# Alternating the row strips of small matmuls, a block-diagonal compression and nested expert conditions in a two-block transformer step

## The chip, the cores and the metric

One Trainium2 chip; the program runs on one core. The metric is the device time of one execution in microseconds (us), the median of several runs.

## The reference

One sequence of 256 tokens of width 1024 goes through two blocks, all in float32.

The first block adds a mix of two branches (a two-direction RWKV-7 scan over a context of 256 tokens and then the sequence; a two-dimensional neighbourhood attention) and then a mixture of 16 experts, of which each token takes two. The second block is two layers. Each projects its input to the operands of four branches, mixes their outputs by gates and adds a feed-forward step over a table of 128 x 128 experts. Two of the four branches matter here:

```
# sparse attention: 15 compressed keys and values, from 32 tokens each
tok = jnp.arange(n_cmp)[:, None] * CMP_STRIDE + jnp.arange(CMP_LEN)[None, :]
def compress(kv, w):
    blk = kv[:, tok] + cmp_pos
    return blk.reshape(B, n_cmp, CMP_LEN * Dh) @ w
kc = compress(k_cmp, cmp_wk)
vc = compress(v_cmp, cmp_wv)
...
# gated linear attention (GLA): 4 heads, 32 wide, chunked
att = jnp.einsum('bhtk,bhsk,bhtsk->bhts', qi, ki, decay)
intra = jnp.einsum('bhts,bhsv->bhtv', att, vi)
```

In the first block, the RWKV step needs, per head of width 64, the products of decayed keys with decayed keys and queries within chunks of 64 tokens.

## The kernel before

**Weights and products.** All weights stream from memory in float32, in units of 128 x 1024 (512 KB). Class `Stream` loads each unit into a tile wf (4 buffers, all loads issued by SyncE, SP in the profile, in the program's order) and splits it in two fp32r parts: wh by ScalarE, wl by VectorE or GpSimd. A dense product is then three matmuls (`mm3`, lines 418 to 420: high by high, low by high, high by low). Matmuls in plain float32, as the attention branches use them, leave two LDWEIGHTS and two MATMUL records each in the trace.

**Row strips.** A matmul whose contraction is 64 or 32 rows uses the strip of the array at its operands' partitions: head p in partitions 64p to 64p + 63, or, for GLA, head h in 32h to 32h + 31.

**Order.** Functions are generators; `interleave` (from line 340) runs them in turn, a step to each yield. In `layer` (around line 1690) three run side by side: the dense projections (za, zt, zb, zc and then the gate weights mg), one lane with stick-breaking and then sparse attention (`nsa`), one lane with `gla` and then retention. A lane waits until `self.ready` counts the projections that it needs; `ready` is 7 when the last, zc, is there. The framework's own scheduler then decides the order of instructions on each engine, so neighbours in the code need not stay neighbours on TensorE.

**The places of the change.**
- `rw_prep` (first block, L1050): for each of two strips p four matmuls into one bank, then masks by VectorE (L1053), then the next strip; behind both, transposes (L1057). It is called 16 times; in half of them the moving operand is 64 wide, in half 128.
- `moe`: the experts run with 64 slots each (`SLOTS`). Then a count n, the most tokens of one expert, is loaded to registers of all engines, and three conditions in a row (L1360: n over 64, 128, 192) guard three further passes; with the inputs here n is not over 64 and none is entered. Behind them mx = accumulated output x m5 (L1372) is added to x (L1374), and the layer norm (L1603) and transposes (L465) start the second block.
- `gla`: per head and per half tt of the tokens, 8 matmuls of 32 rows (L1869, one of the eight L1867) into banks 4 and 5, four to a bank; two multiplies by masks (L1872) and a sum (L1873); then a cross product (L1876).
- `nsa`: the compression weights cw (128 x 32 x 64, keys in partitions 0 to 63, values in 64 to 127) come in one load; per token offset j two matmuls accumulate: keys (L1920, 64 rows by 64, 15 moving columns, bank 2) and values (L1921, 64 rows by 15, 64 moving columns, bank 3). ScalarE copies the keys to kcb (L1925), VectorE the values to vcb (L1927). Further down the scores of the selected and window keys (L1976) loop over strip p, then over b.

## Time and profile before

| | |
|---|---|
| median of 3 runs | 3157.56 us (3152.04 to 3164.92) |
| the profiled execution | 3153.57 us |
| its span, first to last instruction | 3151.8 us, 52665 instructions |
| mean granted TensorE clock | 0.966 of full speed |
| TensorE (PE) busy | 2972.6 us, 94% |
| its weight loads (PEld) busy | 2544.3 us, 81% |
| VectorE (DVE) busy | 2028.2 us, 64% |
| ScalarE (ACT) busy | 1411.4 us, 45% |
| GpSimd (POOL) busy | 382.0 us, 12% |
| read from memory | 548.62 MB, 174 GB/s over the span |

The profile is of one execution. Its times are from the start of the span. Busy times of TensorE come from modelled ends of matmuls: starts that follow each other tell the pitch. [...] An "L" with a number is a line of the kernel before. Names: bank is an accumulator bank; X are GLA's decayed operands; blk the windows of 15 x 32 tokens; KBT and KRT the RWKV operands.

### The profile page before, as it was taken

To read this page: it belongs to the slowest core of one execution; us is meant where nothing else is said; L and a number is where in the kernel's file an instruction comes from. 1 tells how busy PE (TensorE), PEld (TensorE's weight loads), DVE (VectorE), ACT (ScalarE), POOL (GpSimd) and SP (SyncE) were. 2 spreads that over 40 slices of the span, in tenths; PEclk is the share of its full clock that TensorE was granted. 3 is DMA by queue.
4 is the path that set the end of the run, shared out by engine and by line. 5 is a ranking of instruction groups with operands and counts; after the bars stand their busy time and mean duration, and the time that the engine had idled before them with its cause. 6 is when DMAs were issued, how large, how long until landed. Compare 5 with 4: busy or idle time off the path is not lost. (4 is left out here: it accounts for less than half of the span.)

```text
span 3151.8 us, 52665 instructions
## 1 busy us (share of the span) xinstructions
PE 2972.6 (94%) x20690; PEld 2544.3 (81%) x20690; DVE 2028.2 (64%) x3822; ACT 1411.4 (45%) x2488; POOL 382.0 (12%) x334
## 2 busy tenths in 40 slices
PE   7999958899699989999999999999999999999998
PEld 5789647544388979999998888789889999988886
DVE  3568586311265577968986666664669868976666
ACT  4555433211254544444544555553444445445553
POOL 1110131000101051320010000110413310010000
PEclk9999968999899999999999999998999999999999
DMA  6333516699332444554445555533454554456665
GB/s 229 127 95 116 196 38 252 269 409 408 130 124 101 156 154 156 174 181 155 155 168 196 193 193 193 186 117 101 159 165 154 168 167 157 156 186 192 193 193 159
DMA packets 159134, 553.29 MB, mean 176 GB/s; under 512 B 19442, under 2 KB 25748, under 8 KB 157588
## 3 DMA queue, kind: packets, MB, share of 16 engines
q1 hardware_dynamic: 158868, 549.74, 50.6%
q8 instruction: 168, 2.75, 0.4%
q14 instruction: 98, 0.80, 0.1%
HBM read 548.62 MB, written 1.05 MB: 174 GB/s over the span
## 5 line engine op out<-in xcount | busy, mean ns | idle before, releaser
L337 DVE TENSOR_TENSOR wl<-wf,wh 128x1024 fp32r<-128x1024 f32 x690 | 865.9, 1255 | 402.2 <-ACT wh L336 401.4
L336 ACT CAST wh<-wf 128x1024 fp32r<-128x1024 f32 x745 | 778.6, 1046 | 682.0 <-PE bank L419 475.0
L420 PE MATMUL bank<-xth,wl 128*128 128x256 f32 x3040 | 869.5, 287 | 18.9 <-DVE wl L337 15.4
L418 PE MATMUL bank<-xth,wh 128*128 128x256 f32 x3040 | 884.6, 291 | 2.8 <-ACT B L2075 1.5
L419 PE MATMUL bank<-xtl,wh 128*128 128x256 f32 x3040 | 867.8, 286 | 2.9 <-DVE xtl L477 2.9
L420 PEld LDWEIGHTS bank<-xth,wl 128*128 128x128 f32 x3040 | 588.2, 194 | 23.1 <-DVE wl L337 17.7
L418 PEld LDWEIGHTS bank<-xth,wh 128*128 128x128 f32 x3040 | 588.7, 194 | 10.8 <-issue 2.1
L419 PEld LDWEIGHTS bank<-xtl,wh 128*128 128x128 f32 x3040 | 589.2, 194 | 4.3 <-DVE xtl L477 3.7
L419 PE MATMUL bank<-wl,gh 128*128 128x512 f32 x1024 | 399.0, 390 | 3.5 <-DVE wl L337 3.5
L420 PE MATMUL bank<-wh,gll 128*128 128x512 f32 x1024 | 396.2, 389 | 0.0
L418 PE MATMUL bank<-wh,gh 128*128 128x512 f32 x1024 | 278.2, 389 | 3.2 <-ACT gh L413 3.2
L413 ACT CAST gh<-B 128x256 fp32r<-128x256 f32 x256 | 103.6, 407 | 340.5 <-PE bank L419 340.5
L419 PEld LDWEIGHTS bank<-wl,gh 128*128 128x128 f32 x1024 | 192.2, 188 | 45.0 <-DVE wl L337 5.2
L418 PEld LDWEIGHTS bank<-wh,gh 128*128 128x128 f32 x1024 | 192.2, 188 | 43.6 <-ACT gh L413 3.6
L420 PEld LDWEIGHTS bank<-wh,gll 128*128 128x128 f32 x1024 | 192.2, 188 | 39.7
L414 DVE TENSOR_TENSOR gll<-B,gh 128x256 fp32r<-128x256 f32 x256 | 116.9, 459 | 130.1 <-ACT gh L413 127.4
L337 POOL TENSOR_TENSOR wl<-wf,wh 128x1024 fp32r<-128x1024 f32 (+1 forms) x55 | 153.1, 2786 | 312.0 <-ACT wh L336 303.8
L1445 PE MATMUL bank<-raw,xe 128*64 128x512 f32 x512 | 130.1, 600 | 0.0
L2280 DVE TENSOR_TENSOR eq<-iota,picks 128x1024 f16<-128x1024 f16 x128 | 89.4, 699 | 47.1 <-PE bank L2292 45.7
L506 POOL TENSOR_TENSOR x<-x,r_ln 128x1024 f32<-128x1024 f32 x12 | 34.8, 2930 | 500.1 <-DMA r_ln<-in_rows 489.4
L1445 PEld LDWEIGHTS bank<-raw,xe 128*64 128x64 f32 x512 | 37.2, 136 | 66.0 <-issue 64.2
L2281 DVE TENSOR_TENSOR gm<-eq,picks 128x1024 f16<-128x1024 f16 x128 | 88.6, 693 | 0.0
(588 smaller groups left out, 4370.1 us busy)
## 6 DMA issues: line engine op xcount, KB each, us to landing
wf<-in_pu SPq DMA_DIRECT2D x256, 512.0 KB, 3.5
wf<-in_pv SPq DMA_DIRECT2D x256, 512.0 KB, 4.2
raw<-in_w SPq DMA_DIRECT2D x192, 512.0 KB, 10.1
wf<-in_mg SPq DMA_DIRECT2D x64, 512.0 KB, 3.5
mw<-in_modw SPq DMA_DIRECT2D x48, 512.0 KB, 4.6
wf<-in_win_t SPq DMA_DIRECT2D x37, 512.0 KB, 3.6
wf<-in_wq SPq DMA_DIRECT2D x32, 512.0 KB, 3.6
wf<-in_zt SPq DMA_DIRECT2D x28, 512.0 KB, 3.3
```

The costliest lines, as they stand in the source:

```text
L336: nc.scalar.copy(h[:, :w], src[:, :w])
L337: (nc.gpsimd if gpsimd else nc.vector).tensor_sub(lo[:, :w], src[:, :w], h[:, :w])
L413: self.nc.scalar.copy(h, src)
L414: return self.nc.vector.tensor_sub(lo, src, h)
L418: mm(out, lh, rh, start=start, stop=False)
L419: mm(out, lh, rl, start=False, stop=False)
L420: return mm(out, ll, rh, start=False, stop=stop)
L506: nc.gpsimd.tensor_tensor(self.x[:, tt], self.x[:, tt], gb[:, a:a + D], op=op)
L1445: nc.tensor.matmul(self.ps[j][half[e]], v[p]["x"][:, kk, half[e]], w[j][e][:, c], start=kk == 0, stop=kk == KC - 1)
L2280: nc.vector.tensor_tensor(e, iota[:, None, None].to_broadcast(big), of(0), op=OP.is_equal)
L2281: nc.vector.tensor_tensor(g, e[:, :, 1:2].to_broadcast(big), of(1), op=OP.mult)
```

## The change

Three parts.

- **Heads in turn.** `rw_prep` takes both banks first and alternates the strip with each matmul; `gla` takes heads in pairs, one bank for each head of the pair, and alternates them with each matmul, with the multiplies of both heads behind; the score loop in `nsa` has strip p inside. In `gla` a wait for `ready` = 7 stands before the last step.
- **Compression as one product.** cw is padded on the host to a block-diagonal 128 x 128 per offset (2 MB per layer instead of 1), comes in four loads of eight offsets through two buffers, and 32 matmuls of 128 rows and 15 moving columns give keys and values in one bank. The values, now as 64 x 15, are copied out by VectorE (vt) and transposed by TensorE before the copies to vcb.
- **Conditions nested.** The second condition stands inside the first, the third inside the second (`beyond`).

```
-        o[f"cw_{l}"] = np.concatenate([i[n][l].reshape(32, 64, 64).transpose(1, 0, 2)
-                                       for n in ("nsa_cmp_wk_2", "nsa_cmp_wv_2")], 0)
+        o[f"cw_{l}"] = np.concatenate([np.pad(i[n][l].reshape(32, 64, 64).transpose(1, 0, 2), ((0, 0), (0, 0), (64 * q, 64 - 64 * q)))
+                                       for q, n in enumerate(("nsa_cmp_wk_2", "nsa_cmp_wv_2"))], 0)
...
+                pas = [bank().rearrange("p (c t) -> p c t", c=4) for _ in range(2)]
+                for c in range(4):
+                    for p in range(2):
+                        h = slice(p * 64, p * 64 + 64)
+                        nc.tensor.matmul(pas[p][:, c, :W], flat(KBT[h, c]), flat(KRT[h, c]), start=True, stop=True)
                 for p in range(2):
-                    h = slice(p * 64, p * 64 + 64)
-                    pa = bank().rearrange("p (c t) -> p c t", c=4)
-                    for c in range(4):
-                        nc.tensor.matmul(pa[:, c, :W], flat(KBT[h, c]), flat(KRT[h, c]), start=True, stop=True)
+                    h, pa = slice(p * 64, p * 64 + 64), pas[p]
...
-        for lo in range(SLOTS, T, SLOTS):
-            with tc.If(n > lo), tc.tile_pool(name=f"ex{lo}", bufs=1) as ep:
...
+        self.beyond(n, SLOTS)
...
+    def beyond(self, n, lo):
+        nc, tc = self.nc, self.tc
+        with tc.If(n > lo):
+            with tc.tile_pool(name=f"ex{lo}", bufs=1) as ep:
...
+            if lo + SLOTS < T:
+                self.beyond(n, lo + SLOTS)
...
+        for h0 in range(0, 4, 2):
+            rows = [slice(h * 32, h * 32 + 32) for h in (h0, h0 + 1)]
+            atts = [sp.tile([128, 3, 128], F32, name="att", bufs=2) for _ in rows]
             for tt in range(2):
                 t = slice(tt * 128, tt * 128 + 128)
+                tmps = [sp.tile([128, 8, 128], F32, name="tmp", bufs=2) for _ in rows]
                 for q in range(2):
+                    pq = [self.bank(4, 5).rearrange("p (a b) -> p a b", a=4) for _ in rows]
                     for j in range(4):
                         lv = 4 * q + j
+                        for pp, r in zip(pq, rows):
+                            if lv == at[tt][7]:
+                                nc.tensor.matmul(pp[:, j], kT[r, t], qT[r, t], start=True, stop=True)
+                            else:
+                                nc.tensor.matmul(pp[:, j], X[tt][r, lv], X[tt][r, lv], start=True, stop=True)
+                    yield
+                    for pp, tmp in zip(pq, tmps):
+                        nc.vector.tensor_tensor(tmp[:, 4 * q:4 * q + 4], pp, gm[:, 4 * q + 1 - tt:4 * q + 5 - tt], op=OP.mult)
...
+        while self.ready < 7:
+            yield
...
-        cw = self.load(sp, "cw", A[f"cw_{l}"])
+        some = lambda j: self.load(sp, "cw", A[f"cw_{l}"][:, j:j + 8], bufs=2)
+        cw = [some(0), some(8)]
...
         for j in range(32):
-            nc.tensor.matmul(pk[0:64, 0:15], cw[0:64, j], blk[0:64, j], start=j == 0, stop=j == 31)
-            nc.tensor.matmul(pv[64:79, 0:64], blk[64:128, j], cw[64:128, j], start=j == 0, stop=j == 31)
+            nc.tensor.matmul(pk[:, 0:15], cw[j // 8][:, j % 8], blk[:, j], start=j == 0, stop=j == 31)
             if j % 8 == 7:
+                if len(cw) < 4:
+                    cw.append(some(8 * len(cw)))
                 yield
+        vt = sp.tile([128, 15], F32, name="vt")
+        nc.vector.tensor_copy(vt[64:128], pk[64:128, 0:15])
...
+        nc.tensor.transpose(pv[0:15, 0:64], vt[64:128], self.ident[64:128, 64:128])
+        yield
         for h in range(4):
-            nc.vector.tensor_copy(vcb[h * 32:h * 32 + 15, h], pv[64:79, 0:64])
+            nc.vector.tensor_copy(vcb[h * 32:h * 32 + 15, h], pv[0:15, 0:64])
...
-                for p in range(2):
-                    for b in range(2):
+                for b in range(2):
+                    for p in range(2):
```

The change adds lines, so that a line of the kernel before has a higher number in it: the dense products 418 to 420 are 419 to 421, 1869 is 1880, 1920 and 1921 are 1939.

Three places show how the order of instructions moves. The first is TensorE's order in the first layer's GLA. A row is a line, an operation, its bank and operands, and "x3" three alike in a row; X0 and X1 are the two halves of the tokens. Before, the products of one head in the first half, dense products around them:

```order
L420 MATMUL bank1_62<-xth_10348,wl_10891 128x256
L1763 MATMUL bank6_67<-zA_10344,att_10875 128x64
L1869 MATMUL bank4_65<-X0_10586 128x128
L1764 MATMUL bank6_67<-zA_10344,att_10875 128x64
L1765 MATMUL bank6_67<-zA_10344,att_10875 128x64
L1869 MATMUL bank4_65<-X0_10586 128x128 x3
L1869 MATMUL bank5_66<-X0_10586 128x128 x3
L1867 MATMUL bank5_66<-zT_10347 128x128
L418 MATMUL bank0_61<-xth_10348,wh_10936 128x256
```

After, a group of the first pair of heads; bank 4 is the even head's, bank 5 the odd one's:

```order
L1880 MATMUL bank4_65<-X0_10586 128x128
L1880 MATMUL bank5_66<-X0_10586 128x128
L1880 MATMUL bank4_65<-X0_10586 128x128
L1880 MATMUL bank5_66<-X0_10586 128x128
L1880 MATMUL bank4_65<-X0_10586 128x128
L1880 MATMUL bank5_66<-X0_10586 128x128
L1880 MATMUL bank4_65<-X0_10586 128x128
L1880 MATMUL bank5_66<-X0_10586 128x128
L420 MATMUL bank1_62<-xtl_10349,wh_10907 128x256
```

and another of the same pair, in the second half of the tokens:

```order
L1774 MATMUL bank6_67<-zA_10344,att_10738 128x64
L1880 MATMUL bank4_65<-X1_10587 128x128 x4
L419 MATMUL bank1_62<-xth_10348,wh_10822 128x256
L420 MATMUL bank1_62<-xtl_10349,wh_10822 128x256
L1880 MATMUL bank5_66<-X1_10587 128x128 x4
L421 MATMUL bank1_62<-xth_10348,wl_10823 128x256
```

One group alternates the heads with each product, the other has the two heads apart with dense products between. In all a layer has, by strip, the groups 000, 11101, 00110101, 00001111, 0000, 1111, 23232323 and three times 22233323.

The second place is TensorE's order in the compression of the first layer. Before, keys (bank 2) and values (bank 3) alternate:

```order
L1921 MATMUL bank3_64<-cw_11433,blk_11435 15x64 x4
L1920 MATMUL bank2_63<-blk_11435,cw_11433 64x15
L1921 MATMUL bank3_64<-cw_11433,blk_11435 15x64
L1920 MATMUL bank2_63<-blk_11435,cw_11433 64x15
L1921 MATMUL bank3_64<-cw_11433,blk_11435 15x64
L1920 MATMUL bank2_63<-blk_11435,cw_11433 64x15
L1921 MATMUL bank3_64<-cw_11433,blk_11435 15x64
```

After, the 32 products stand in chunks of 1, 9, 2, 12 and 8 with dense products between; two of the chunks:

```order
L1757 MATMUL bank3_64<-lm_11311,c_ones_10842 128x128
L1939 MATMUL bank2_63<-blk_11440,cw_11436 128x15 x7
L1939 MATMUL bank2_63<-blk_11440,cw_11438 128x15 x2
L419 MATMUL bank0_61<-xth_10348,wh_11288 128x256
...
L421 MATMUL bank1_62<-xth_10348,wl_11359 128x256
L1939 MATMUL bank2_63<-blk_11440,cw_11438 128x15 x4
L1939 MATMUL bank2_63<-blk_11440,cw_11462 128x15 x8
L1774 MATMUL bank6_67<-zB_10345,att_11466 128x64
```

The third is SP's order of loads in the first layer, after the change (before, one load of cw, 128x2048, stands at the front and none further down):

```order
L386 DMA cpos<-in_cpos 128x32
L386 DMA cw<-in_cw 128x1024 x2
L284 DMA wf<-in_za 128x824 x4
...
L284 DMA wf<-in_mg 128x1024 x3
L386 DMA cw<-in_cw 128x1024
L284 DMA wf<-in_mg 128x1024 x3
L386 DMA cw<-in_cw 128x1024
L284 DMA wf<-in_mg 128x1024 x23
```

Two loads of cw stand ahead of the layer's weights, as the one did, and two among the gate weights mg.

## Rows read from the trace of the kernel before

**Rows 1.** The page's table of engines: busy us, share of the span, instructions.

```profile
PE 2972.6 (94%) x20690; PEld 2544.3 (81%) x20690; DVE 2028.2 (64%) x3822; ACT 1411.4 (45%) x2488; POOL 382.0 (12%) x334
```

**Rows 2.** Stretches in us: their length, busy us by engine (instructions), PEclk, DMA share, GB/s.

```profile
890.00:930.00 40.00, 40.00 (x252) 33.73 (x251) 29.28 (x48) 20.69 (x31) 2.20 (x3) 1.00 0.33 112
...
970.00:1010.00 40.00, 40.00 (x285) 33.00 (x284) 14.50 (x28) 12.71 (x22) 3.14 (x5) 0.83 0.26 90
...
2110.00:2152.00 42.00, 42.00 (x279) 35.27 (x280) 14.34 (x27) 11.90 (x21) 3.13 (x5) 0.77 0.27 85
```

**Rows 3.** Waits from 857 to 1112, SP's queue and PE: total us, times, longest.

```profile
SPq L283 <- DVE wl L337: 170.7, 45, 14.3
...
PE bank L418 <- ACT xth L476: 1.4, 1, 1.4
```

**Rows 4.** Timeline behind the experts: start us, us, engine, instruction, [idle before, releaser].

```profile
843.63 2.48 DVE L1372 TENSOR_TENSOR mx<-bank,m 128x512 f32<-128x512 f32 x4 [17.02 <-PEq L1360]
...
851.14 1.09 PE L465 MATMUL bank<-c_ident,x 128*128 128x128 f32 x4 [23.63 <-DVE x L1603]
```

**Rows 5.** The conditions' line: engine, operation, ns min/median/max, first and last start us.

```profile
L1360 PEldq COMPARE_BRANCH x3: 4553/4656/6046, 827.7 to 838.8; - x3
L1360 SPq COMPARE_BRANCH  x3: 45/45/50, 828.2 to 838.4; - x3
L1360 PEldq EVENT_SEMAPHORE x3: 51/51/51, 833.8 to 843.5; - x3
```

**Rows 6.** Stretches, instructions with cw alone: PE and PEld busy, PEclk, DMA, GB/s.

```profile
971.00:1006.00 35.00, 15.71 (x128) 10.40 (x128) 0.85 0.30 102
2110.00:2146.00 36.00, 14.94 (x128) 9.97 (x128) 0.82 0.32 99
```

**Rows 7.** Timeline of PE in the compression (operands: weights' partitions*columns, moving).

```profile
990.08 0.39 PE L1920 MATMUL bank<-blk,cw 64*64 64x15 f32 x2
990.40 0.39 PE L1921 MATMUL bank<-cw,blk 64*15 64x64 f32 x2
...
1001.39 0.28 PE L1920 MATMUL bank<-blk,cw 64*64 64x15 f32 x2
...
1004.80 0.70 PE L1788 MATMUL bank<-zT 64*128 64x256 f32 x2
```

**Rows 8.** Timeline of PE's weight loads, the expert gate product.

```profile
780.43 0.52 PEld L1432 LDWEIGHTS bank<-gate,P 128*128 128x128 f32 x4
```

**Rows 9.** Weight loads by source line: ns min/median/max, first and last start us.

```profile
L1920 PEld LDWEIGHTS bank<-blk,cw x128: 128/133/224, 971.7 to 2144.4; 64*64 64x64 f32 x128
L1921 PEld LDWEIGHTS bank<-cw,blk x128: 87/92/112, 980.3 to 2144.7; 64*15 64x15 f32 x128
L1432 PEld LDWEIGHTS bank<-gate,P x32: 188/192/193, 590.9 to 795.9; 128*128 128x128 f32 x32
```

**Rows 10.** Stretches of 4 us beside the compression, as in rows 2.

```profile
996.00:1000.00 4.00, 4.00 (x21) 4.00 (x22) 0.00 (x0) 0.00 (x0) 0.00 (x0) 0.55 0.00 0
...
2152.00:2156.00 4.00, 4.00 (x28) 3.75 (x26) 1.68 (x5) 1.33 (x2) 0.00 (x0) 0.84 0.00 0
```

**Rows 11.** GLA: a stretch with X's instructions alone (as rows 2), and PE's timeline.

```profile
857.00:1112.00 255.00, 16.89 (x120) 14.46 (x120) 4.50 (x30) 2.28 (x4) 0.95 0.38 131
...
937.09 1.72 PE L1869 MATMUL bank<-X 32*128 32x128 f32 x14
938.74 0.39 PE L418 MATMUL bank<-xth,wh 128*128 128x256 f32 x1
```

**Rows 12.** Timeline of PE in the first block's preparation.

```profile
207.19 1.60 PE L1050 MATMUL bank<-KRT,KBT 64*128 64x64 f32 x16
208.72 0.66 PE L1057 MATMUL bank<-c_ident,KBT 128*128 128x128 f32 x4
209.31 1.10 PE L1050 MATMUL bank<-KRT,KBT 64*128 64x64 f32 x8
210.34 0.39 PE L418 MATMUL bank<-hxh,wh 128*128 128x256 f32 x1
```

More of the change, by code (lines that the diff above doesn't have):

```diff
@@ L1358, in moe @@
         n = nc.values_load(count[0:1, 0:1], min_val=0, max_val=T, skip_runtime_bounds_check_because="a count of the tokens")
-        for lo in range(SLOTS, T, SLOTS):
-            with tc.If(n > lo), tc.tile_pool(name=f"ex{lo}", bufs=1) as ep:
-                more = ep.tile([128, SLOTS], F32, name="slots")
-                nc.vector.tensor_scalar(more, self.iota[:, :SLOTS], float(lo + 1), None, op0=OP.add)
-                st = Raw(nc, "", "a" * 6)
-                self.experts_units(st)
-                st.open("a", ep)
-                self.experts(ep, st, more, False)
+        self.beyond(n, SLOTS)
         with tc.tile_pool(name="t2", bufs=1) as tp:
@@ L1375, in moe @@
         self.ms.close()
+    def beyond(self, n, lo):
+        nc, tc = self.nc, self.tc
+        with tc.If(n > lo):
+            with tc.tile_pool(name=f"ex{lo}", bufs=1) as ep:
+                more = ep.tile([128, SLOTS], F32, name="slots")
+                nc.vector.tensor_scalar(more, self.iota[:, :SLOTS], float(lo + 1), None, op0=OP.add)
+                st = Raw(nc, "", "a" * 6)
+                self.experts_units(st)
+                st.open("a", ep)
+                self.experts(ep, st, more, False)
+            if lo + SLOTS < T:
+                self.beyond(n, lo + SLOTS)
     def experts_units(self, st):
@@ L1853, in gla @@
         po = self.ps[6].rearrange("p (t c) -> p t c", t=2)
-        for h in range(4):
-            r = slice(h * 32, h * 32 + 32)
-            att = sp.tile([128, 3, 128], F32, name="att", bufs=2)
+        for h0 in range(0, 4, 2):
+            rows = [slice(h * 32, h * 32 + 32) for h in (h0, h0 + 1)]
+            atts = [sp.tile([128, 3, 128], F32, name="att", bufs=2) for _ in rows]
             for tt in range(2):
                 t = slice(tt * 128, tt * 128 + 128)
-                tmp = sp.tile([128, 8, 128], F32, name="tmp", bufs=2)
-                pq = []
+                tmps = [sp.tile([128, 8, 128], F32, name="tmp", bufs=2) for _ in rows]
@@ L1861, in gla @@
                 for q in range(2):
-                    pp = self.bank(4, 5).rearrange("p (a b) -> p a b", a=4)
-                    pq.append(pp)
+                    pq = [self.bank(4, 5).rearrange("p (a b) -> p a b", a=4) for _ in rows]
                     for j in range(4):
                         lv = 4 * q + j
-                        if lv == at[tt][7]:
-                            nc.tensor.matmul(pp[:, j], kT[r, t], qT[r, t], start=True, stop=True)
-                        else:
-                            nc.tensor.matmul(pp[:, j], X[tt][r, lv], X[tt][r, lv], start=True, stop=True)
@@ L1870, in gla @@
-                yield
-                for q in range(2):
-                    nc.vector.tensor_tensor(tmp[:, 4 * q:4 * q + 4], pq[q], gm[:, 4 * q + 1 - tt:4 * q + 5 - tt], op=OP.mult)
-                nc.vector.tensor_reduce(att[:, 2 * tt], tmp.rearrange("p a b -> p b a"), axis=AX.X, op=OP.add)
-                yield
-            pp = self.bank(4, 5)
-            nc.tensor.matmul(pp[:, 0:128], X[0][r, at[0][7]], X[1][r, at[1][7]], start=True, stop=True)
+                        for pp, r in zip(pq, rows):
[3 more added lines that the diff above has]
+                                nc.tensor.matmul(pp[:, j], X[tt][r, lv], X[tt][r, lv], start=True, stop=True)
@@ new lines, in gla @@
+                    yield
+                    for pp, tmp in zip(pq, tmps):
+                        nc.vector.tensor_tensor(tmp[:, 4 * q:4 * q + 4], pp, gm[:, 4 * q + 1 - tt:4 * q + 5 - tt], op=OP.mult)
+                for att, tmp in zip(atts, tmps):
+                    nc.vector.tensor_reduce(att[:, 2 * tt], tmp.rearrange("p a b -> p b a"), axis=AX.X, op=OP.add)
+                yield
+            pq = [self.bank(4, 5) for _ in rows]
+            for pp, r in zip(pq, rows):
+                nc.tensor.matmul(pp[:, 0:128], X[0][r, at[0][7]], X[1][r, at[1][7]], start=True, stop=True)
@@ L1877, in gla @@
             yield
-            nc.scalar.copy(att[:, 1], pp[:, 0:128])
+            for pp, att in zip(pq, atts):
+                nc.scalar.copy(att[:, 1], pp[:, 0:128])
             yield
-            vs = slice(h * 64, h * 64 + 64)
-            self.causal_out(po[:, :, vs], att.rearrange("p a b -> p (a b)"), v, vs)
+            for h, att in zip((h0, h0 + 1), atts):
+                vs = slice(h * 64, h * 64 + 64)
+                self.causal_out(po[:, :, vs], att.rearrange("p a b -> p (a b)"), v, vs)
```

1 line of the change is left out of this document (added).

## The prediction

> **What bounds the kernel now.** The first view is the page's table of busy time by engine: TensorE is busy in 2972.6 of 3151.8 us [rows 1], so only two kinds of edit can pay: one that shortens TensorE's own work where it never rests, and one that shortens a stretch in which it stands still. Both kinds are here. The table by stretches, second, tells where TensorE never rests: in the stage of both second-block layers in which the dense projections run beside the four attention branches it is busy 40.00 of 40 us, 42.00 of 42, while VectorE is at 29.28 of 40 or less [rows 2]; the gated-linear-attention (GLA) and compression products of the change lie there. In that stage of the first layer, TensorE's waits add up to 1.4 us [rows 3]. So a product that gets shorter there shortens the span, until something else is late. The third view, by source line, and the timeline behind it show the other kind: after the experts TensorE stands still for 23.63 us [rows 4], and in this time each engine passes three conditions whose bodies are not entered (no expert has more than 64 tokens here).
>
> The sum is made against the profiled execution, 3153.57 us, which is 4.0 us under the median of the runs shown, 3157.56. A measurement of this kernel can tell about 0.5% from no change, 15.8 us.
>
> **The three conditions.** Before, an engine jumps over a body three times. TensorE's three compare-and-branch records last 4.55, 4.66 and 6.05 us, and its last one begins at 838.8; its last semaphore step is at 843.5, its first at 833.8 [rows 5]. The product mx, on VectorE, waits 17.02 us for TensorE's sequencer and starts at 843.63; x, the layer norm and the transposes follow on it, and TensorE resumes at 851.14 [rows 4]. Nested, a false outer condition skips all three at once: one jump. VectorE is then released after the first of the three, at 833.8 and some 0.6 for the records that remain, 834.4 in place of 843.63: **-9.2**. The rest of that chain moves as it is. Bounds: if the one longer jump costs twice a short one, -4.6; if the cheapest of three stays, 4.55, -9.7 or so. What would be late next is the weight queue, which jumps too; its own three branches begin at 828.2 to 838.4 [rows 5] and lose two jumps with the rest.
>
> What a jump costs is read from these rows. [...]
>
> **The compression.** Per layer 64 products (keys and values, 32 each), two records each, alternate between two tile shapes; with their groups' ends they keep TensorE busy for 15.71 us in the first layer and 14.94 in the second [rows 6]. At full clock a product takes 0.21 us (16 from 1001.39 to 1004.80), at half clock 0.32 (990.08 to 990.40) [rows 7]. Now 32 products remain, of one full shape, with 15 moving columns. The nearest row is the gate product of 128x128 by 2 columns: four loads in 0.52 us [rows 8], one of them lasting 0.19 [rows 9], so that the pitch is (0.52 - 0.19) / 3 = 0.11 per record. So 64 x 0.11 = 7.0 us, and 0.4 for the one new transpose with its change of shape: 7.4 per layer. 15.71 + 14.94 - 2 x 7.4 = **-15.8**. Bounds: if all ran at half clock, 0.21 per record, 13.9 per layer, -3; at 0.09, the median length of the shorter load now [rows 9], -18. The added copy and four copies from another bank are VectorE's, which has room [rows 2].
>
> **The clock around it.** [...] I take half of the loss as won back: **-5**, bounds 0 and -11.
>
> **GLA.** Per layer 64 products of 32 rows, two records each; the 56 of them that read X, with four cross products, keep TensorE busy 16.89 us [rows 11]. Before, one head's products come in a row, all in the same strip of rows: 14 records begin at 937.09 and the dense product behind them at 938.74, 1.65 us, 0.11 each once the change of shape is off [rows 11]. That two strips can overlap is seen in the first block: a group of 16 records on two strips, eight and eight, takes 1.53 us (207.19 to 208.72), a half by itself 1.03 (209.31 to 210.34), so that one border already saves 0.5 [rows 12]. Eight products that alternate fully, at half the pitch, would save 0.9. But the order on TensorE alternates only partly: of the groups in a layer one alternates fully, three have a late second head, some stay on one strip or meet at one border. Pricing each so gives -4.0 per layer, **-8**; bounds 0 (no overlap at 128 columns) and -15 (all at half the pitch). The pairing needs both banks for one step; VectorE's multiplies come in pairs as before.
>
> **The smaller products of two strips.** In the first block's preparation, 16 calls of 16 records: by the order about ten now alternate, each 0.5 better than the one border before, and two more than before are split apart, each 0.5 worse [rows 12]: **-4**, bounds +3 and -8 (VectorE and GpSimd lead in part of that stage). The selected and window scores swap two loops; one call of four is split more often, priced as above: **+0.5**, bounds -1.5 and +1.8. The cross products stay single: 0.
>
> **What is added.** The padded compression weights are 2 MB per layer instead of 1, in four loads through two buffers; the third and fourth wait for products, and 3 and then 23 loads of mg weights stand behind them on SP's queue. That queue already stops for up to 14.3 us in this stage, with TensorE waiting 1.4 us in all [rows 3]. I put **+1** there, bounds 0 and +5. The wait for seven finished projections before the last GLA step holds no engine by itself: 0.
>
> Sum: -9.2 - 15.8 - 5 - 8 - 4 + 0.5 + 1 = -40.5; 3153.6 - 40.5 = 3113, and with the 4.0 to the median **3117 us**.
>
> **The rivals.**
> 1. *Strips don't overlap when two heads alternate*: GLA 0, preparation +1, scores +0.5. For it: in GLA no row before shows two strips side by side. Against it: the border of 0.5 us [rows 12]. The sum then is -27.5: 3130.
> 2. *All the overlap and the whole clock*: -15, -8 and -11 in place of -8, -4 and -5: 3100. For it, the dense work between the new chunks; against it, the clock also falls after a short run. [...]
> 3. *A product is paid by its load.* The two loads of 64 and 15 columns last 133 and 92 ns, the one of 128 columns 192 [rows 9]; a pair of products then went from 450 to 384 ns, and 32 of them save 2.1 us per layer: -4.2 in place of -15.8: 3129. Against it: records follow each other at 0.11 in either shape, however long the load [rows 7, 8]. [...]
> 4. *The nesting saves nothing*: the outer jump lies over three bodies and stalls as long as three jumps did. Against it: each engine's code shows one taken jump. 3126.
> 5. *SP's queue becomes the bound*, the one that ends slower. Each of the four late loads, waiting for eight products of the same layer, holds TensorE for as long as the queue's longest stop, 14.3 us [rows 3], on top of what the weights on hand cover: 57 us, so 3117 + 57 = 3174. It decides from the point where a stop outlasts those weights, over 14.3 us by the same row. Against it: stops up to that length cost TensorE nothing before, and few products stand ahead of each late load.
>
> **How the numbers follow.** My sum 0.60, the rivals 0.14, 0.12, 0.07, 0.04 and 0.03. The range runs from just under rival 2 to just above rival 1 without the clock's gain (3135): 3097 to 3137. Rivals 1 to 4 each end under 3141.8, which is 0.5% below the median: faster 0.93; the same 0.04, where three of them come together or rival 5 costs half; slower 0.03.
>
> **What would show it.** After: one long branch on TensorE, and mx waiting some 8 us for its sequencer in place of 17.02; compression busy near 7.5 us per layer; GLA's products from X near 13; a clock above 0.83 and 0.77 in the last two stretches of [rows 2]; TensorE still without waits in that stage. The prediction is wrong if TensorE waits on SP's loads there, if a 128-row product takes 0.3 us or more, or if GLA stays at 16.9.

## The result and the profile after

| | before | changed | |
|---|---|---|---|
| median, in alternation on one chip | 3161.24 us (3152.04 to 3169.94, 4 runs) | 3119.28 us (3113.76 to 3123.59, 4 runs) | ratio 0.9871, 95% interval 0.9844 to 0.9898 |
| median, on another chip later | 3164.6 us (3161.3 to 3173.7, 9 runs) | 3116.0 us (3114.32 to 3119.9, 5 runs) | ratio 0.9844, 0.9830 to 0.9857 |
| the profiled execution | 3153.57 us | 3123.59 us | 3114.32 us in the later trace (e9) |

The change makes the kernel 1.3% to 1.6% faster, 42.0 us on the first chip and 48.6 us on the later one; forecast were 3117 us, in 3097 to 3137. The two profiled executions are 30.0 us apart and not 42: the one of before is among the quickest of its runs, the one of after the longest of its four. So the accounts below are made by stretches.

The page of the changed kernel:

```profile
PE 2952.4 (95%) x20564; PEld 2530.2 (81%) x20564; DVE 2032.1 (65%) x3824; ACT 1413.0 (45%) x2488; POOL 389.1 (12%) x334
```

Beside [rows 1], TensorE has 126 records and 20.2 us less; of 20690 it lost 128 by the compression's halving, and two came for the new transposes. The other engines' busy times are as they were within 2%.

**Where the time went.** The program is cut at products that both kernels have: the last expert product, the first transpose behind it (L465), the first dense product of a layer (bank<-wh,xth), the first and the last product of the mix (operands oh, ol). The times are starts in the timelines; the lengths are their differences, in us. The first column runs from the first product of KRT and KBT to the last expert product. "Lanes" is the stage of a layer in which the dense projections and the attention branches run side by side, "mix" the products behind it that combine the four branches; e1 to e12 are the experiments.

| kernel | preparation to experts | experts to transposes | lanes 1 | mix 1 | lanes 2 | mix 2 |
|---|---|---|---|---|---|---|
| before | 619.9 | 24.0 | 250.7 | 32.5 | 253.2 | 33.5 |
| changed | 613.7 | 14.9 | 238.8 | 34.8 | 235.5 | 39.7 |
| changed, e9 | 613.6 | 14.8 | 236.5 | 34.0 | 235.4 | 38.9 |
| e1 nesting alone | 620.1 | 14.4 | 252.3 | 33.7 | 253.1 | 35.0 |
| e2 compression alone | 624.7 | 24.4 | 240.0 | 39.0 | 239.5 | 38.6 |
| e3 GLA alone | 619.0 | 24.6 | 244.9 | 32.3 | 244.2 | 34.2 |
| e4 strips alone | 614.8 | 24.3 | 250.7 | 33.9 | 252.9 | 34.1 |
| e5 strict alternation | 617.0 | 14.9 | 235.2 | 34.1 | 237.9 | 34.0 |
| e6 first split of the mix | 614.8 | 15.4 | 236.2 | 32.7 | 235.3 | 34.6 |
| e7 small chunks | 613.7 | 15.2 | 232.8 | 43.5 | 233.9 | 46.3 |
| e8 all three | 613.8 | 14.9 | 233.4 | 45.5 | 233.4 | 47.6 |
| e10 strict, first split | 613.7 | 15.0 | 235.1 | 33.5 | 238.4 | 32.8 |
| e11 as e10, chunks of four | 616.6 | 15.0 | 235.1 | 33.2 | 236.2 | 35.4 |
| e12 as e10, chunks of two, lane of three | 618.0 | 14.7 | 233.3 | 32.5 | 234.1 | 33.3 |

The lanes got 11.9 and 17.7 us shorter, the stop behind the experts 9.1, the first block 6.2; the mix behind the lanes got longer, 2.3 and 6.1 us. What is left, 856.6 us behind the first mix and 854.7 behind the second up to the last product, is 1.2 and 3.2 us longer in the trace of the changed kernel, and differs by as much between traces of kernels that are the same there: that is how far a single trace can be off. The mixes drift too: in before, e1, e3 and e4, where they are the same, they last 32.3 to 35.0 us. So the first mix's 34.8 and 34.0 (e9) show no change; the second's 39.7 and 38.9 do.

**The conditions.** The view by source line, and the timeline behind the experts (columns as in [rows 4, 5]):

```profile
L1377 PEldq COMPARE_BRANCH  x1: 5752/5752/5752, 824.4 to 824.4; - x1
L1377 PEldq EVENT_SEMAPHORE  x1: 51/51/51, 830.2 to 830.2; - x1
```

```profile
831.16 2.48 DVE L1369 TENSOR_TENSOR mx<-bank,m 128x512 f32<-128x512 f32 x4 [7.90 <-SPq L1377]
...
838.67 1.94 PE L466 MATMUL bank<-c_ident,x 128*128 128x128 f32 x8 [14.52 <-DVE x L1614]
```

One long jump of 5.75 us is left on TensorE. mx waits 7.90 us in place of 17.02, TensorE 14.52 in place of 23.63 [rows 4]: 9.1 less for both, so that the chain behind moved as it is. What releases mx last is now SP's queue, 0.6 us behind TensorE's sequencer (830.8 and 830.2).

**The compression.** Stretches with cw's instructions alone (as [rows 6]) and TensorE's timeline:

```profile
950.00:990.00 40.00, 8.13 (x64) 8.28 (x64) 0.91 0.44 142
2080.00:2118.00 38.00, 7.48 (x64) 7.64 (x64) 0.96 0.48 150
```

```profile
957.15 2.08 PE L1939 MATMUL bank<-blk,cw 128*128 128x15 f32 x18
...
970.69 3.40 PE L1939 MATMUL bank<-blk,cw 128*128 128x15 f32 x24
980.52 1.85 PE L1939 MATMUL bank<-blk,cw 128*128 128x15 f32 x16
```

15.71 and 14.94 us became 8.13 and 7.48. A chunk of 18 records takes 2.08 us, one of 16 takes 1.85: (2.08 - 1.85) / 2 = 0.115 each, with loads of 128 columns. The chunk of 24 took 3.40 us since the clock fell within it, and stayed down for what followed (stretches, as [rows 2]; PEclk, third from the end, is the share of its full clock that TensorE was granted):

```profile
972.00:980.00 8.00, 8.00 (x41) 7.66 (x41) 1.74 (x3) 0.14 (x1) 0.00 (x0) 0.57 0.39 132
980.00:988.00 8.00, 8.00 (x67) 7.69 (x66) 3.13 (x9) 2.99 (x6) 0.00 (x0) 1.00 0.21 68
```

One such stretch of 8 us is left in the first layer, 0.57 from 972 to 980, near the 0.50 that before has from 992 to 996; in the second layer the lowest is 0.79, from 2102 to 2110. Before, it was below 0.85 in 24 us of the first layer's compression (988 to 1012) and 32 of the second's (2120 to 2152).

**GLA.** The stretch with X's instructions alone, and two pieces of TensorE's timeline:

```profile
844.00:1088.00 244.00, 13.71 (x120) 11.26 (x120) 4.48 (x30) 2.29 (x4) 0.97 0.42 142
```

```profile
902.43 1.15 PE L1880 MATMUL bank<-X 32*128 32x128 f32 x8
...
914.06 1.16 PE L1880 MATMUL bank<-X 32*128 32x128 f32 x16
```

Eight records of one head take 1.15 us, 16 records of two heads in turn take 1.16: two neighbours on different strips start 0.01 us apart, and the next two follow 0.11 us later. They overlap wholly. Since only some groups alternate, X's busy time fell from 16.89 us [rows 11] to 13.71.

**The preparation.** L1050 before, L1052 after, alone from 205 to 428 us:

```profile
205.00:428.00 223.00, 32.32 (x256) 29.05 (x256) 0.93 0.38 126
```

```profile
205.00:428.00 223.00, 24.53 (x256) 21.14 (x256) 0.96 0.41 129
```

**What was given back.** TensorE's waits in the mix of the second layer, before (2210 to 2320) and after (2205 to 2300), and SP's queue in the first layer's lanes after (as [rows 3]):

```profile
PE bank L418 <- DVE mt L2029: 4.8, 2, 3.3
...
PE bank L420 <- POOL wl L337: 1.3, 1, 1.3
```

```profile
PE bank L421 <- POOL wl L338: 4.7, 1, 4.7
PE bank L419 <- DVE mt L2054: 4.4, 2, 3.5
```

```profile
SPq L284 <- DVE wl L338: 157.9, 47, 8.0
...
SPq L386 <- PE bank L1939: 6.8, 2, 4.3
```

The late loads of cw do stop SP's queue, for 4.3 us at most; its longest stop there is 9.6 us, put down to the added copy vt, where it was 14.3 before. TensorE waits for no weights within the lanes. The stop is behind them: in the mix TensorE waits 4.7 us for a weight's low part made by GpSimd (line 337 before, 338 now). GpSimd's timeline there, before and after:

```profile
2243.95 11.59 POOL L506 TENSOR_TENSOR x<-x,r_ln 128x1024 f32<-128x1024 f32 x4 [10.69 <-DMA wf<-in_wbr]
2255.51 2.37 POOL L337 TENSOR_TENSOR wl<-wf,wh 128x1024 fp32r<-128x1024 f32 x1
```

```profile
2209.81 10.43 POOL L507 TENSOR_TENSOR x<-x,r_ln 128x1024 f32<-128x1024 f32 x4 [12.24 <-DMA wf<-in_wbr]
2220.19 3.32 POOL L338 TENSOR_TENSOR wl<-wf,wh 128x1024 fp32r<-128x1024 f32 x1
```

Four products of the layer norm, over 10 us on GpSimd, wait for loads and stand ahead of that split. The mix begins at 2250.48 before and at 2211.91 after: the norm's products had begun 6.5 us ahead of it, and now 2.1.

This wait is 3.4 us longer than before; the second mix is 6.1 us longer. Part of the rest is the clock. Both mixes as stretches (as [rows 2]), before and after:

```profile
1108.10:1140.60 32.50, 24.82 (x195) 23.43 (x194) 27.22 (x29) 10.21 (x14) 26.62 (x13) 1.00 0.37 132
2250.50:2284.00 33.50, 27.36 (x195) 26.28 (x194) 27.80 (x30) 10.22 (x14) 27.58 (x13) 0.90 0.38 128
```

```profile
1083.70:1118.60 34.90, 28.62 (x196) 27.23 (x195) 29.43 (x31) 10.44 (x14) 28.10 (x13) 0.86 0.39 132
2211.90:2251.60 39.70, 30.57 (x206) 28.83 (x205) 31.63 (x34) 12.24 (x17) 30.87 (x15) 0.87 0.37 122
```

The second mix now lacks 0.13 of 39.70 us, 5.2 us, where before it lacked 0.10 of 33.50, 3.4 us: some 2 us more. But in e1, e3 and e4, whose mixes are those of before, the clock there is 0.86 to 1.00, so that these traces don't tell how much of this the change brought.

### The profile page after: what moved, and what is told of

Same layout as the page of the kernel before. It is cut to its first block, busy times and chain, and to the rows that moved or that the text cites. A ratio compares the mean times of both kernels' runs of the same rounds, so it can differ in the third digit from the quotient of the medians.

```text
span 3121.8 us, 52406 instructions
## 1 busy us (share of the span) xinstructions
PE 2952.4 (95%) x20564; PEld 2530.2 (81%) x20564; DVE 2032.1 (65%) x3824; ACT 1413.0 (45%) x2488; POOL 389.1 (12%) x334
## 5 line engine op out<-in xcount | busy, mean ns | idle before, releaser
L419 PEld LDWEIGHTS bank<-xth,wh 128*128 128x128 f32 x3040 | 589.2, 194 | 10.7 <-issue 2.7
```

The source lines that it names most:

```text
L419: mm(out, lh, rh, start=start, stop=False)
```

## The experiments

The first four are the kernel before with one part of the change each, on one chip with 12 runs of the kernel before (median 3162.1 us).

### e1: the nesting alone

```
-        for lo in range(SLOTS, T, SLOTS):
-            with tc.If(n > lo), tc.tile_pool(name=f"ex{lo}", bufs=1) as ep:
...
+        self.beyond(n, SLOTS)
```

with `beyond` as in the change.

> The kernel before with the three conditions nested and nothing else. Theory (two of three jumps over a body are saved, the chain behind moves as it is): mx starts 9 to 10 us earlier behind the last expert product (8.1 us after its start instead of 17.2), the whole span is 9 to 10 us shorter and nothing else in the trace moves by more than 1 us. Rival (what the nested form saves is taken back by a later stop, as the queue of weights is the late one): mx earlier, but the first dense product of the second block less than 5 us earlier.

Measured: 3150.71 us, ratio 0.9965 (0.9951 to 0.9979), 11.4 us less. The timeline behind the experts:

```profile
834.47 2.48 DVE L1365 TENSOR_TENSOR mx<-bank,m 128x512 f32<-128x512 f32 x4 [7.39 <-SPq L1373]
841.98 1.94 PE L465 MATMUL bank<-c_ident,x 128*128 128x128 f32 x8 [14.01 <-DVE x L1610]
```

TensorE stands still 14.01 us in place of 23.63, 9.6 less, and the first dense product follows as before, 6.26 us behind the transposes. The theory holds, the rival falls. Not as expected: stretches that this kernel shares with the one before are up to 1.6 us longer in its trace, which in sum hides over half of the gain there (the two traces are 3.7 us apart); the medians and the stretch show it.

### e2: the compression alone

```
-        cw = self.load(sp, "cw", A[f"cw_{l}"])
+        some = lambda j: self.load(sp, "cw", A[f"cw_{l}"][:, j:j + 8], bufs=2)
+        cw = [some(0), some(8)]
...
-            nc.tensor.matmul(pk[0:64, 0:15], cw[0:64, j], blk[0:64, j], start=j == 0, stop=j == 31)
-            nc.tensor.matmul(pv[64:79, 0:64], blk[64:128, j], cw[64:128, j], start=j == 0, stop=j == 31)
+            nc.tensor.matmul(pk[:, 0:15], cw[j // 8][:, j % 8], blk[:, j], start=j == 0, stop=j == 31)
```

with the padded weights, the loads further down and the transpose, as in the change.

> The kernel before with the compression as one block-diagonal product and nothing else. Theory: 64 records of 0.11 us per layer, TensorE busy on cw near 7.8 us per layer instead of 15.7 and 14.9, and 6 to 8 us more from the clock beside it: the two stages of dense projections and lanes are together 20 to 24 us shorter. Rival A (the clock has nothing to do with it, it falls as before): 14 to 16 us. Rival B (loads of cw waiting for their buffers stop the weights): TensorE waits for weights of over 3 us in these stages, and the gain is under 12 us.

Measured: 3146.09 us, ratio 0.9952 (0.9933 to 0.9970), 16.0 us less. The lanes are 10.7 and 13.7 us shorter, 24.4 together, just above the theory's 20 to 24: cw's products account for 14.7 of it (8.15 and 7.76 us). The granted clock over the lanes, 0.95 and 0.95 before and 0.99 and 0.98 here, makes some 18 us by their lengths, more than the other 9.7; rival A falls. What took the difference is open. But the mixes are 6.5 and 5.1 us longer. TensorE's waits in the second mix:

```profile
PE bank L421 <- POOL wl L338: 5.2, 1, 5.2
PE bank L419 <- DVE mt L2038: 4.1, 2, 3.5
```

The wait for GpSimd is 5.2 us, and 4.0 in the first mix, beside 1.3 and 1.7 before. The norm's products begin 2.9 and 1.1 us ahead of the mix (1101.95 to 1104.81, 2238.46 to 2239.57). So by kernel and layer, lead and wait go together: 6.0 and 1.7, 6.5 and 1.3 before; 5.9 and 1.8, 2.1 and 4.7 after; 5.8 and 1.9, 2.9 and 3.9 in e9; 2.9 and 4.0, 1.1 and 5.2 here. The waits explain 6.2 us of the mixes' 11.6; their clock is 0.87 and 0.91, where it was 1.00 and 0.90. Rival B falls too: TensorE waits 0.5 us for a load of cw in the first layer's lanes and for no other weights there. That something is given back was right, but its place is the mix.

### e3: GLA alone

```
-        for h in range(4):
...
+        for h0 in range(0, 4, 2):
...
```

with the heads in pairs and the wait for `ready`, as in the change.

> The kernel before with GLA's heads in pairs and nothing else. Theory (neighbouring products on different strips overlap): products that read X keep TensorE busy 13.5 to 14 us per layer instead of 16.9, and the two stages are together 5 to 8 us shorter. Rival (the products of different strips don't overlap, what was gained in the changed kernel came from fewer changes of tile shape): in a group of eight products that alternate, records still follow each other at 0.11 us and the busy time stays above 16 us.

Measured: 3147.09 us, ratio 0.9959 (0.9934 to 0.9983), 15.0 us less. X alone, first layer:

```profile
855.00:1108.00 253.00, 13.71 (x120) 11.26 (x120) 4.47 (x30) 2.29 (x4) 0.95 0.40 133
```

The busy time is that of the changed kernel, 3.2 us less per layer, and a group of 16 in turn takes 1.16 us: the rival falls. The lanes got shorter by more than that, 5.8 and 9.0 us, in sum 14.8 where 5 to 8 were expected; the clock beside the compression, which this kernel has as before, fell less in its trace: in the second layer it is 1.00 in two of the four stretches of 8 us from 2120 to 2152, and 0.88 and 0.70 in the others, where before it was 0.79, 0.80, 0.71 and 0.50. Why it did is open.

### e4: the preparation and the scores alone

```
+                for c in range(4):
+                    for p in range(2):
+                        h = slice(p * 64, p * 64 + 64)
+                        nc.tensor.matmul(pas[p][:, c, :W], flat(KBT[h, c]), flat(KRT[h, c]), start=True, stop=True)
...
-                for p in range(2):
-                    for b in range(2):
+                for b in range(2):
+                    for p in range(2):
```

in `rw_prep` and in the scores of `nsa`, as in the change.

> The kernel before with the two small loop swaps alone: the first block's preparation and the selected and window scores. Theory: the preparation's products keep TensorE busy 24 to 26 us instead of 32.3 and the first block ends 4 to 7 us earlier, part of it by a clock that falls less in the last 30 us of the scan; the scores change by less than 1.5 us. Rival (the scan's end is set by VectorE and by the clock, not by these products): the first block ends within 2 us of before.

Measured: 3155.49 us, ratio 0.9976 (0.9961 to 0.9990), 6.6 us less. The preparation's products keep TensorE busy 27.16 us (205 to 430), a little above the theory, and the way from them to the last expert product takes 614.8 us, 5.1 less. Over all traces it is 613.6 to 618.0 where the swap is in and 619.0 to 624.7 where it isn't. The rival falls. The lanes, with the scores in them, are as before within 0.4 us.

The four together, 11.4 + 16.0 + 15.0 + 6.6 = 49.0, are near what the whole change gave in e9, 48.6; in the first comparison it gave 42.0. The four intervals are 9 to 16 us wide each, so that this sum bears out both and doesn't show that the parts add up to the us.

The next four are the changed kernel with something more (kernel before: 3162.76 us on that chip).

### e5: strict alternation

```
-                            if lv == at[tt][7]:
-                                nc.tensor.matmul(pp[:, j], kT[r, t], qT[r, t], start=True, stop=True)
-                            else:
-                                nc.tensor.matmul(pp[:, j], X[tt][r, lv], X[tt][r, lv], start=True, stop=True)
+                            a, b = (kT[r, t], qT[r, t]) if lv == at[tt][7] else (X[tt][r, lv], X[tt][r, lv])
+                            with self.tc.issue_after(last.ins) if last else nullcontext():
+                                last = nc.tensor.matmul(pp[:, j], a, b, start=True, stop=True)
```

and so in the preparation and the scores.

> The changed kernel with an order edge from each small product to the next one of the other strip, so that GLA, the preparation and the scores alternate strictly (all but a first product that stands alone in most groups). Theory (neighbours on two strips overlap, the changed order leaves some of it unused): products that read X go from 13.7 to some 11 to 12.5 us per layer, and the whole is 2 to 6 us shorter than the changed kernel. Rival (what is left of the overlap is eaten by one more change of tile shape per group): X no lower than 13 us, the same time.

Measured: 3116.51 us, ratio 0.9853 (0.9836 to 0.9869). X alone, and two groups of it:

```profile
835.00:1085.00 250.00, 13.13 (x120) 9.88 (x120) 4.49 (x30) 2.29 (x4) 0.96 0.44 148
```

```profile
883.76 0.48 PE L1880 MATMUL bank<-X 32*128 32x128 f32 x2
885.99 1.15 PE L1880 MATMUL bank<-X 32*128 32x128 f32 x14
```

13.71 became 13.13 only. The groups alternate, but in seven of eight the first product goes by itself, and it takes 0.48 us, where the 14 records behind it take 1.15. In two of these its bank comes free first: VectorE's multiplies of the group before end at 904.92 and 905.51, the lone product begins at 904.97 and the other seven at 905.93. In four more both banks were free before the first product, and the order alone sets it apart. The rival holds in its number, X no lower than 13 us; that a change of shape makes the lone product's time is not shown. The time is that of the changed kernel: 0.9853 lies between its own two ratios, 0.9871 and 0.9844.

One thing moved that was not looked for. The norm's products begin 5.9 and 5.8 us ahead of the two mixes, TensorE waits 1.8 and 1.9 us for GpSimd's split, and the mixes last 34.1 and 34.0 us: the second layer's stop went by the order alone, with the split where it was. The second layer's lanes took 2.4 us more, beside a clock of 0.57 from 2102 to 2110 (0.79 in the changed kernel).

### e6: the first split of the mix on VectorE

```
-            self.st.pool_every = MIX_POOL
             for d in range(8):
+                self.st.pool_every = MIX_POOL if d else 0
```

> The changed kernel with the first split in the mix behind the lanes moved from GpSimd to VectorE; nothing else. Theory (part of the gain is given back there: the dense stage ends earlier, but the layer norm's four products on GpSimd, 10 to 12 us, wait for a late load and stand ahead of that split): TensorE's waits for GpSimd's wl, 1.8 and 4.7 us in the two layers, go, and the whole is 4 to 7 us shorter than the changed kernel. Rival (the next wait ends at the same time, the mix is bound by VectorE or by GpSimd's later work): waits move to VectorE's wl or mt and the time stays within 2 us.

Measured: 3116.84 us, ratio 0.9849 (0.9832 to 0.9865). TensorE's waits in the second mix:

```profile
PE bank L419 <- DVE mt L2054: 6.8, 2, 3.5
PE bank L466 <- DVE x L1614: 2.3, 2, 1.2
PE bank L420 <- DVE xtl L478: 1.4, 2, 1.0
...
PE bank L421 <- DVE wl L338: 0.4, 1, 0.4
```

The wait for GpSimd is gone; 2.4 us of it came back as a wait for mt. The mixes last 32.7 and 34.6 us, near 32.5 and 33.5 before; together that is 7.2 less than in the changed kernel's first trace and 5.6 less than in e9's. So the stop there is that one split behind the norm's products: it goes when the split is moved, as it goes in e5 when the norm's products start earlier. The 4 to 7 us that were expected of the whole are not shown: 0.9849, too, lies between the changed kernel's 0.9871 and 0.9844.

### e7: compression in small chunks

```
-            if j % 8 == 7:
-                if len(cw) < 4:
-                    cw.append(some(8 * len(cw)))
+            if j % 8 == 7 and len(cw) < 4:
+                cw.append(some(8 * len(cw)))
+            if j % 2:
                 yield
```

> The changed kernel with a step boundary after every second compression product, so that the 32 products of a layer stand in chunks of at most five instead of 9, 12 and 8, with dense products between; nothing else. Theory (the clock falls behind a long unbroken run of these products): the granted clock stays at 0.95 or above in every 8 us of the compression's stretch, and the two stages are 3 to 6 us shorter. Rival (the clock falls for another reason): it falls as in the changed kernel, 0.57 to 0.85 over some 4 to 8 us per layer, and the time is the same or up to 2 us longer by the changes between products.

Measured: 3126.34 us, ratio 0.9885 (0.9869 to 0.9902): longer than the changed kernel (0.9844, 0.9830 to 0.9857, in e9; against its first 0.9871 the intervals overlap). The clock did as the theory has it: it is 1.00 in every 8 us from 948 to 1004 and from 2070 to 2126, among them the one in which it was 0.57 in the changed kernel:

```profile
972.00:980.00 8.00, 8.00 (x66) 7.79 (x66) 2.98 (x4) 2.66 (x4) 0.00 (x0) 1.00 0.43 135
```

and the lanes are, with those of e8, the shortest of all, 232.8 and 233.9 us. But with 12 steps more the lane of the sparse attention ends later than the dense products, and the mix, which needs its output, waits (second mix; 10.9 us in the first). The last transposes of that lane, and the wait:

```profile
2217.34 0.55 PE L1721 MATMUL bank<-c_ident,o 128*128 128x128 f32 x3 [0.29 <-POOL o L2031]
```

```profile
PE bank L419 <- DVE mt L2054: 10.4, 3, 6.3
```

They begin 5.0 us behind the mix's first product (2212.31); in the changed kernel they stand 11.8 us ahead of it (2200.08 and 2211.91).

The mixes grew to 43.5 and 46.3 us. The theory is right on the clock and wrong on the time; neither it nor the rival had the lane's end.

### e8: the three together

The three edits above on the changed kernel.

> The three edits before this one together on the changed kernel: strict alternation, the first split of the mix on VectorE, compression in small chunks. If each pays and they add up: 9 to 18 us shorter than the changed kernel, 3101 to 3110 us on a chip on which that has 3119. If they overlap (the stage's end is then set by the lanes): 4 to 8 us.

Measured: 3127.52 us, ratio 0.9885 (0.9868 to 0.9901), a miss of both: mixes of 45.5 and 47.6 us. With the late lane the other two edits give nothing.

The last four ran on one chip (kernel before: 3164.6 us).

### e9: the change again

> The changed kernel itself, on the same chip as the three after it, so that they are compared with it directly: 0.985 to 0.990 of the kernel before.

Measured: 3116.0 us (3114.32 to 3119.9), 0.9844 (0.9830 to 0.9857), a little under what was expected. Against this the next three stand.

### e10: strict alternation and the first split

The edits of the two sections above, without the small chunks.

> The changed kernel with strict alternation and with the first split of the mix on VectorE, the compression's chunks as in the change. If the two gains (4 to 7 us each by the runs before) add up: 8 to 13 us shorter than the changed kernel. If both were worth the same stop at the end of the lanes: 4 to 7 us.

Measured: 3112.42 us (3111.69 to 3119.65), 0.9834 (0.9818 to 0.9850): 3.6 us less than e9, under both sizes that were expected, and the runs overlap, so that a gain is not shown. The mixes are back at 33.5 and 32.8 us; the second layer's lanes took 238.4, beside a clock of 0.61 from 2102 to 2110, behind an unbroken run of 16 compression products (2099.26).

### e11: chunks of four, two steps less

```
+            if j % 4 == 3:
                 yield
...
             nc.scalar.copy(kcb[p * 64:p * 64 + 64, p, 0:15], pk[0:64, 0:15])
-        yield
         nc.tensor.transpose(pv[0:15, 0:64], vt[64:128], self.ident[64:128, 64:128])
-        yield
```

on the kernel of e10.

> The kernel of the run before with a step boundary after every fourth compression product and two boundaries less behind the compression, so that chunks are of 5 to 8 products and the sparse attention still ends some 85 TensorE rows ahead of the mix's first product. Theory (the clock's part of the small chunks is kept, and without a late lane the stop in the mix doesn't come): clock 0.95 or above beside the compression, waits for mt as in the changed kernel (under 6 us a layer), 3 to 6 us shorter than the run before. Rival (chunks of 8 are long enough for the clock to fall): the clock falls to 0.6 to 0.9 in one or two stretches of 8 us per layer and the time is within 3 us of the run before.

Measured: 3116.02 us (3113.3 to 3119.14), 0.9839 (0.9825 to 0.9852). The stop in the mix didn't come (33.2 and 35.4 us), but the clock fell behind two chunks of eight products, in both layers:

```profile
980.00:988.00 8.00, 8.00 (x57) 7.79 (x56) 1.85 (x3) 1.33 (x2) 0.00 (x0) 0.82 0.46 160
...
2110.00:2118.00 8.00, 7.99 (x54) 7.69 (x53) 1.85 (x3) 1.33 (x2) 0.00 (x0) 0.81 0.46 141
```

The rival holds on the clock; the time is 3.6 us over the run before, with ranges that overlap, where it had at most 3.

### e12: chunks of two, three steps of the lane to a round

```
-                interleave((dense(), 1), (la, 2), (second(), 2))
+                interleave((dense(), 1), (la, 3), (second(), 2))
```

with the boundary after every second product, on the kernel of e10 (strict alternation and the first split).

> The kernel of the run before the last with a boundary after every second product and three steps of that lane to a round instead of two, so that the lane ends earlier and not later. Theory: clock 0.95 or above, no stop at the mix, 3 to 8 us shorter than strict alternation and mix alone. Rival (three steps to a round take VectorE and the weights' splits at the wrong time): TensorE waits for wl in the stage, and it is no shorter or some us longer.

Measured: 3109.67 us (3106.23 to 3111.89), 0.9820 (0.9806 to 0.9834). All its runs are under all runs of the changed kernel on that chip, 6.3 us by the medians; against e10, which has neither chunks nor lane, it is 2.8 us, and the ranges touch. The clock stays at 1.00 in every 8 us from 948 to 1012 and from 2070 to 2134, one of which is

```profile
2102.00:2110.00 8.00, 8.00 (x64) 7.35 (x63) 4.58 (x13) 2.70 (x5) 0.00 (x0) 1.00 0.24 71
```

and no wait for wl stands among TensorE's in the lanes; the mixes last 32.5 and 33.3 us. The theory holds for the clock and for the stop; its 3 to 8 us against e10 are not shown. This version is faster than both kernels. One of its chunks has ten products (961.24, 20 records in 2.30 us) and the clock didn't fall behind it, nor behind those of nine (957.15) and eight (980.52) in the changed kernel, while it fell behind chunks of eight in e11: the length of a chunk alone doesn't settle it.

## Why the prediction was right

It was right: 3117 us forecast, 3119.28 and 3116.0 measured, 3097 to 3137 the range. That the time was hit to 1 or 2 us is in part luck: the forecast of the change was -40.5, and it gave -42.0 and -48.6, from a kernel before that was 4 to 7 us slower in these comparisons (3161.24, 3164.6) than in the three runs that the forecast started from (3157.56). Step by step, in us; the lanes' and mixes' lengths are from the table by stretches, the rest from the rows above.

| step | forecast | measured in the changed kernel |
|---|---|---|
| two jumps less | -9.2 | -9.1; alone -9.6 |
| compression | -15.8 | 8.13 + 7.48 - 15.71 - 14.94 = -15.0 |
| GLA | -8 | 2 x (13.71 - 16.89) = -6.4 |
| scores | +0.5 | 12.4 - 11.6 = +0.8 busy |
| the clock | -5 | lanes -29.6, less the three above: -9.0 |
| preparation | -4 | -6.2; busy -7.8 |
| what is added | +1 | no wait for weights in the lanes; mixes +8.4 |

- **The jumps.** Right in size and in mechanism: one jump left, and the whole chain moves. The wait for mx is 7.90 us where some 8 was forecast; that SP's queue, and not TensorE's sequencer, would end it was not foreseen and cost nothing to speak of. Rival 4 falls. The one long branch left lasts 5.75 us, where the three before lasted 4.55 to 6.05; what a branch spends this time on was not shown.
- **The compression.** Right: the record's pitch is that of the gate product, 0.115 for 0.11, and half the records go. Rival 3, that a product is paid by the columns of its load, falls: twice the columns in a load, the same pitch, 0.115 with 128 columns and 0.213 for two records with 64 or 15.
- **The clock.** Right in direction, low in size. No run shows the -5 as such, half of a loss of 11: it was a choice without a row behind it. What the runs showed in its place is -9.0, nearly twice as much, within the bounds of 0 and -11. The -9.0 is a remainder; the granted clock over the lanes, 0.95 and 0.95 before and 0.97 and 0.98 after, makes it some 13 us with the compression's own part. The loss was under-read: before, thirteen stretches of 4 us beside the compression are below 1.00 (nine of them below 0.80), and they lack 17.1 us, of which 15.71 + 14.94 - 128 x 0.213 = 3.4 are the compression's own.
- **GLA and the preparation.** Right in kind: two strips overlap, wholly (16 records in 1.16 us, 8 in 1.15), as the border in the preparation had hinted. For GLA the order's partly alternating groups gave 3.2 us per layer of the 4.0 counted; for the preparation 6 in place of 4. Rival 1 falls. Rival 2, all of the overlap and the clock, didn't come. The strict order should have brought the rest of the overlap and didn't either: a lone first product in seven of eight groups takes it.
- **What is added.** The step that failed: "I put **+1** there, bounds 0 and +5". No weights are late in the lanes; the late loads of cw stop the queue for 4.3 us at most, and rival 5 falls. What is late next is GpSimd in the mix, with its norm's products ahead of a split, a place that the sum had no term for, since the split lies behind the stage that was shortened. In the second layer, and in both when the compression stands alone, that is 3.9 to 5.2 us of waiting where it was 1.3 and 1.7. With the split moved (e6) it is gone, and with an earlier start of the norm's products (e5) it is 1.9. The rest of the second mix's +6.1 is in part clock and in part open. The first mix's +2.3 is not of this kind: its wait is 1.8 us as before (1.7), the clock fell there to 0.83 from 1090 to 1100, and the mixes of before differ by as much.

The measured column adds up to -36.5; the two traces differ by -30.0, with 2.9 us lost ahead of the preparation (its first product starts at 207.19 [rows 12] and at 210.1) and 4.4 behind the mixes up to the last product, in work that is the same, and 0.7 won behind that. So two of the sum's terms are off by 4 and 7 us in opposite ways, by single traces that drift by a few us, and the range covered it.

## What to carry to other kernels

Where TensorE never idles, count records and their pitch: halving the number of small products by padding them to a full one, and letting neighbours use different strips of rows, both paid here at the price read from the trace, and again through a clock that fell less (0.97 and 0.98 over the lanes, 0.95 before). Look behind the stage that gets shorter for work that starts by a load or on another engine, not by the stage's end, and write down its lead: here some 6 us of lead left a wait of 1.3 to 2.1 us, and 1 to 3 us one of 3.9 to 5.2 us. A lane beside a bound engine may not get more steps than it has slack: 12 steps more made the lanes 5 to 8 us shorter and the mixes 15 to 17 us longer.

## What had not been expected of the hardware

- Products of two 32-row strips in turn overlapped wholly, in float32 with 128 moving columns: 16 records in 1.16 us, 8 on one strip in 1.15.
- At full clock a float32 record of 15 to 64 moving columns kept its pitch here, some 0.11 us, whether its load had 15 or 64 columns (0.213 us for two, before) or 128 (0.115, after).
- The granted clock fell behind chunks of twelve products of the compression (in the changed kernel 0.57 from 972 to 980, 0.79 from 2102 to 2110) and, in e11, of eight (0.82 and 0.81); it stayed at 1.00 behind one of ten in e12 and behind those of nine and eight in the changed kernel. In e7 and e12, with a boundary after every second product, it stayed at 1.00 in every 8 us from 948 to 1004 and from 2070 to 2126. What decides it was not settled.
